# Shifting the tiles of a two-layer encoder kernel so that the two operands of every wide matmul start at the same offset modulo 512 bytes

## The chip, the cores and the metric

One Trainium2 chip; the program runs on one of its cores. The time is device microseconds of that core for one execution, and three executions of the kernel before are given. A profile of one more execution is read for the reasons.

## The reference, cut to what matters

Two layers over 1024 tokens of 1024 channels, all in float32. Each layer is a token mixer and a channel mixer, each between two RMS norms:

```
for l in range(DEPTH):                      # DEPTH = 2
    h = rmsnorm(x, g_pre_mix[l])
    z = h @ w_in[l]                         # 1024 -> 1536 columns
    y_f = fourier_mix(z[:, :256])           # 2-D DFT over positions and channels
    y_s = spatial_gating(z[:, 256:768])     # u * (W_s layernorm(v) + b), 4 heads, 128-token chunks
    y_a = gqa_attention(z[:, 768:])         # 8 query heads, 2 key/value heads of 64, rotary
    m = concat(rmsnorm(y_f), rmsnorm(y_s), rmsnorm(y_a)) * g_mix @ w_out[l]
    x = x + rmsnorm(m, g_post_mix[l])
    h = rmsnorm(x, g_pre_ffn[l])
    f = (silu(h @ w_gate[l]) * (h @ w_up[l])) @ w_down[l]    # 2816 hidden columns
    x = x + rmsnorm(f, g_post_ffn[l])
```

## The kernel before

Every float32 operand of a large product is kept as a pair (hi, lo) of float32r values, and a product is three matmuls, hi·hi, hi·lo and lo·hi (`matmul3`, line 142 of the profile). `matmul3` issues three times a pair of instructions: a load of a 128x128 stationary operand (the profile's engine PEld) and a matmul that streams a moving operand of 128x512 past it (PE). Nearly all of the kernel's time on the tensor engine is such matmuls. The loads run ahead, under the matmul before.

The stages of a layer, with the name that the profile gives to each stage's result tile:

- `z`: the input projection, three chunks of 512 columns by eight token tiles, 24 matmuls for each. The stationary operand is a piece of `hT` (transposed activations), the moving one a weight pair `w_z`. In the first chunk the transposes of the next token tile (`tp_h`) and of the keys (`ktp`) stand between the matmuls, in the third those of the Fourier and gating groups (`vf`, `yf`, `sv`, `ms`); the second chunk, for the queries, has none.
- attention: for each of 16 groups (token tile, kv head) of a layer and each of 8 key tiles, four transposes of exponentials (`ptr<-identr,pj`), two matmuls `pv<-pT,vv`, and, ahead for the next group, scores `sc<-kT,qT` in fours.
- `m`: the output projection, two runs of 24 matmuls for each token tile with transposes (`ytp`, `tp`) between them.
- gate and up (`fx`, `fy`): Strassen-Winograd products, 14 for each of 11 pairs of hidden tiles (7 variants by gate and up), 12 matmuls each. The stationary operand is a weight pair `w_f`, the moving one a variant of the activations: B11, B21, T1 (tiles `hB11`, `hB21`, `hT1`, on the left side of the memory) or T2, T3, T4, B22 (`hT2`, `hT3`, `hT4`, `hB22`, on the right). Of a pair's 168 matmuls 96 so have their moving operand on the right.
- down (`fX`, `fY`): Strassen-Winograd products whose operands `dw` lie in tiles of either side, with sums on POOL (`dr`), splits on ACT and DVE (`dw`) and accumulation on DVE (`nat`, line 1120).

Memory is given out by pools that grow from the left (low addresses) or the right (high addresses). A tile's size is rounded up to 32 bytes of a partition. Pools opened and closed as stacks reuse the same bytes, and a tile waits for the last use of the tiles that held its bytes. The order of instructions on each engine is set by the code, by `issue_after` constraints, and by the framework's planner (`schedule_with_timeline_sim=True`). The program's own table of tile addresses gives, in bytes of a partition:

```
tile                         address           mod 512   side
w_z, w_f, most w_wo (Wp)     57088 + 4096 i    256       left
raw tiles, first yT (rawp)   93952 + 4096 i    256       left
kT / vv / hB11 / hB21 / hT1  110336 ...        256       left
rf   (pool al)               134912            256       left, 32 bytes
qst, qT (pool al)            134944, 139040 .. 288       left, behind rf
vs, vsp (pool zs)            150336, 154432    320       left, behind rf and sgb
hT (z), hT2..hT4, hB22       163808 ... 212960 480       right
pT, half of the pj, oT       167904 ...        480       right
later yT, yFT, two w_wo      172000 ...        480       right
chm / ut, vt (pool fp)       170944 / 173024.. 448 / 480 right, mean (32 bytes) between
dw (down)                    both sides        256, 480  both sides
```

So the operands of a `z` matmul lie at 480 (stationary) and 256 (moving), those of T2, T3, T4 and B22 at 256 and 480, those of `pv` at 256 and 480, those of `sc` at 288 and 256, those of `m` mostly at 480 and 256, and those of B11, B21 and T1 both at 256. Of a layer's 924 `fX` and `fY` matmuls 624 have both at 256, 216 both at 480, and 84 have them apart, in runs of three.

The small tiles that the change touches: `one` (a column of ones, in pool `cst`), `mean` (a column of 1/256, set on POOL in `f_open`), `sgb` (the gating bias, loaded by SP after `sgg`), and `rf` (reciprocal roots of the Fourier group). `gz` and `gmx` are two rings of two 32-byte tiles in `cst`, each used once in a layer.

Of the kernel before, what the change touches and what calls it, by code (L numbers as in the profile page):

```python
# [27 lines left out]
# every float32 operand is a pair (hi, lo) of float32r values with x = hi + lo exactly;  # L28
# a product is hi.hi + hi.lo + lo.hi
# [3 lines left out]
def dft_constants():  # L33
    """Constants of the shapes alone: DFT factors and rotary angles."""
# [8 lines left out]
    # f > 0: real and imaginary part of the input give the outputs f; f = 0: two real inputs give the outputs 0 and 4  # L43
# [28 lines left out]
    def pair(v, axis):  # L72
        """(hi, lo): float32 constants as two float32r values."""
        v = v.astype(np.float32)
        hi = ((v.view(np.uint32) + np.uint32(0x800)) & np.uint32(0xFFFFF000)).view(np.float32)
        return np.ascontiguousarray(np.stack([hi, v - hi], axis))
# [5 lines left out]
def encoder_kernel(ctx, tc, A, out):  # L82
# [7 lines left out]
    st = pool("st", 6)  # L90
    nat = pool("natp").tile([P, NT, D], F32, name="nat")
# [14 lines left out]
    # besides ps1's four banks, four more as two pairs (key 2) or on their own (key 1)  # L106
# [8 lines left out]
    # ---------------- helpers  # L115
# [4 lines left out]
    def gain_split(w, raw, g):  # L120
        """(hi, lo) pair of raw with its rows scaled by g."""
        nc.scalar.activation(w[:, 0], raw, AF.Copy, scale=g)
        nc.vector.scalar_tensor_tensor(out=w[:, 1], in0=raw, scalar=g, in1=w[:, 0].bitcast(F32), op0=ALU.mult, op1=ALU.subtract)
# [6 lines left out]
    def wsplit(src, shape, name, p=None, **kw):  # L130
        """float32 in SBUF -> (hi, lo) pair."""
        w = (p or Wp).tile([P, 2] + shape, R32, tag="w", name=f"w_{name}", **kw)
        split(w[:, 0], w[:, 1], src)
        return w

    def rows2(w, r0, c0, n):
        """256 rows of a DRAM matrix as [128, 2, n]."""
        return w[r0:r0 + 256, c0:c0 + n].rearrange("(k p) n -> p k n", p=P)
# [16 lines left out]
    def unit_norm(x, n, name, pool=False):  # L155
        """x = x * rsqrt(mean(x^2) + eps), over the whole free range, in place."""
# [11 lines left out]
    def transpose_4(src, dst, o, name):  # L168
        """dst[:, hi/lo, k, o + tok] = src[tok, k*128 + .]^T for 128 tokens and 512 features."""
# [5 lines left out]
    class Residual:  # L175
        """x = src + rmsnorm(nat[:, t]) * gain, to DRAM; nat[:, t] = rmsnorm(x) * pre_gain, or x itself without a pre_gain.
        The columns of half eh are complete first."""
# [50 lines left out]
    class Later:  # L228
        """Work on the tensor engine that is issued some steps after what it depends on."""
# [16 lines left out]
    def behind(*engines):  # L246
        """Work that each of the engines issues after all that it has got so far."""
# [14 lines left out]
    def chain(*step):  # L262
        """A step that each engine issues after the previous step of the chain."""
# [14 lines left out]
    # ---------------- input projection's weights: three chunks of 512 columns  # L278
# [16 lines left out]
    def z_split(l, c, k):  # L295
        """The norm's gain belongs to the rows of the weights."""
# [4 lines left out]
    # ---------------- start  # L301
# [4 lines left out]
    one = cst.tile([P, 1], F32, name="one")  # L306
    nc.gpsimd.memset(one, 1.0)
    junk = cst.tile([P, 512], BF16, name="junk")
# [18 lines left out]
    # reciprocal roots of the tokens' mean squares: the norm before the input projection is applied to its output  # L327
# [24 lines left out]
    for l in range(DEPTH):  # L352
        gmx = cst.tile([P, 8], F32, tag="gmx", name=f"gmx{l}", bufs=2)
        nc.sync.dma_start(gmx, A["g_mix"][l].rearrange("(k p) -> p k", p=P))
        # ---------------- transposed, split activations (nat holds the pre-normalised tokens)
# [15 lines left out]
        # ---------------- input projection  # L371
# [13 lines left out]
        # queries carry the factor -1/8, so that a row's minimum is minus the maximum of its scaled scores  # L385
# [26 lines left out]
        def rope_apply(src, nh, which, t, dst, name, bufs, scale=1.0):  # L412
            """dst = src [P, nh, 64] times scale, normalised per head, gained and rotated."""
# [22 lines left out]
        # positions-mixed channels, keys and values  # L436
# [26 lines left out]
        # 8-point DFT over the token tiles, in place in nat[:, :, 0:256]  # L463
        def dft8():
# [10 lines left out]
            # xf: 0:e0 1:o0 2:e2 3:o2 4:e1 5:o1 6:e3 7:o3  # L475
            tt(t0, xf(0), xf(2), ALU.add)
            tt(t1, xf(0), xf(2), ALU.subtract)          # U2 real
            nc.vector.tensor_copy(xf(2), t1)
            tt(t1, xf(1), xf(3), ALU.subtract)          # -U2 imag
            tt(xf(3), xf(1), xf(3), ALU.add)  # L480
            tt(xf(0), t0, xf(3), ALU.add)               # U0
            tt(xf(1), t0, xf(3), ALU.subtract)          # U4
# [4 lines left out]
            stt(xf(5), t0, SQ, xf(4), ALU.add)          # U1 real  # L487
            stt(xf(7), t0, -SQ, xf(4), ALU.add)         # U3 real
            stt(xf(4), t1, SQ, xf(6), ALU.add)          # -U1 imag
            stt(xf(6), t1, -SQ, xf(6), ALU.add)         # U3 imag  # L490
# [4 lines left out]
        # queries  # L495
# [10 lines left out]
        sgb = zs.tile([P, 4], F32, name=f"sgb{l}")  # L506
        nc.sync.dma_start(sgb, A["sgu_b"][l].rearrange("h p -> p h"))

        # spatial gating: gelu, layer norm of the gate
# [28 lines left out]
        def gate_mul(i, j):  # L538
            """position mixing of token tiles 4i to 4i + 3, heads 2j and 2j + 1."""
# [12 lines left out]
        # position DFT runs between the second half's tiles  # L552
        fst = {}
        rf = al.tile([P, 8], F32, name=f"rf{l}")
# [8 lines left out]
        def f_open():  # L563
# [3 lines left out]
            fst["mean"] = fp.tile([P, 1], F32, name=f"mean{l}")  # L567
            nc.gpsimd.memset(fst["mean"], 1.0 / 256)
# [11 lines left out]
        def f_pos(f):  # L580
            """channel-major position transform; (channel half, real/imaginary, position), for f = 0 of the outputs 0, then 4."""
# [11 lines left out]
        def f_chan(f):  # L593
            """channel transform. The transform of real values at -k is the conjugate of the one at k."""
# [19 lines left out]
        def f_mean(f):  # L614
            """mean squares (+ eps) at the positions of y's two tiles, the same for both channel halves."""
# [15 lines left out]
        # ---------------- attention  # L631
# [5 lines left out]
        def yf_put(f1):  # L637
            """(hi, lo) of the transformed channels at the positions f1 + 8n; of those of a conjugate, backwards."""
# [11 lines left out]
        def y_tp(t, p=None):  # L650
            """transposed, split output of the gates and of the attention of token tile t."""
# [12 lines left out]
        def out_steps(t, oc, ps):  # L664
            """output projection of token tile t, a step for each 128 rows of the weights."""
# [13 lines left out]
        def wo_load(i):  # L679
            """i-th weight tile of the output projection in the order of use; the group norms' gains belong to its rows."""  # L680
# [117 lines left out]
        # scores and exponentials run ahead, by steps of a key tile  # L798
# [59 lines left out]
        # ---------------- output projection, post-norm, residual, pre-norm of the channel mixer  # L858
# [22 lines left out]
        def b_tp(t):  # L881
            """transposes token tile t's halves of the features, in place in nat; first variants of the right-hand operands."""
# [11 lines left out]
            else:  # L894
                nc.vector.tensor_tensor(out=half(u, 0), in0=ps[0], in1=half(u, 0), op=ALU.subtract)     # T1 = B12 - B11
                nc.scalar.copy(half(t, 1), ps[1])
                nc.vector.tensor_tensor(out=half(t, 0), in0=half(t, 1), in1=ps[0], op=ALU.subtract)     # T3 = B22 - B12

        # ---------------- channel mixer, gate and up: one level of Strassen-Winograd on
        # (output halves i0, i1) x (feature halves) x (token halves)  # L900
# [6 lines left out]
        def nb(i, j, u):  # L907
            """right-hand block (feature half i, token half j), token tiles 2u, 2u + 1 of the half."""
            return nat[:, 2 * u + 4 * j:2 * u + 4 * j + 2, i * 512:(i + 1) * 512]

        # variant and its place, and for some the difference that goes there; T4 is kept with the opposite sign
        TV = {"T1": ((0, 0),), "T2": ((0, 0), (1, 1), (0, 0)), "T3": ((0, 1),), "T4": ((1, 0), (1, 0), (0, 0)), "B22": ((1, 1),)}

        def t_sub(v, u, eng=nc.vector):
            """half u of variant v: T2 = B22 - T1, -T4 = B21 - T2."""
# [19 lines left out]
        def ff_sums(n):  # L935
            """Left-hand operands' sums of product n."""
# [7 lines left out]
            elif v == 3:  # L944
                tt(a21, a11, a21, ALU.subtract)         # S3 = A11 - A21
                tt(a11, sums[p, m], a11, ALU.subtract)  # S2 = S1 - A11
            elif v == 6:
                tt(a12, a12, a11, ALU.subtract)         # S4 = A12 - S2
# [12 lines left out]
        # in the order in which the right-hand operands' variants free nat  # L961
        PC = tuple((u, 0) for u in (4, 5, 6, 7, 0, 1, 2, 3)) + tuple((u, 1) for u in range(NT))

        def pc():
            """the next 2 KB slot for partial results, in nat's space."""
# [20 lines left out]
        def ff_post(n):  # L986
# [4 lines left out]
            def finish(key, acc, i, half):  # L991
                """gate or up block = acc + partial; after both, silu(gate) * up goes to DRAM."""
# [26 lines left out]
        # ---------------- channel mixer, down: Strassen-Winograd on (token halves) x (pairs of  # L1019
        # hidden tiles) x (column halves), groups of pairs accumulate in PSUM, then in nat  # L1020
# [11 lines left out]
        def d_raw_slot(gi, n):  # L1032
            """place of the n-th raw tile of group gi."""
            return RING[(12 * gi + n) % len(RING)]

        def d_load(gi, n):
            """n-th raw tile of a group: first tiles of the pairs, then second ones; hidden values, then weights."""
# [13 lines left out]
        def d_blk(gi, pi, side, b):  # L1051
            """quarter block b (row half * 10 + column half) of the left (side 0) or right factor."""
# [4 lines left out]
        def d_sums(gi, v):  # L1057
            for pi in range(len(DGROUPS[gi])):
# [3 lines left out]
                if v == 5:  # L1062
                    tt(a(11), a(11), a(21))             # S3 = A11 - A21
                    tt(a(21), a(21), a(22), ALU.add)    # S1 = A21 + A22
                    tt(w(11), w(12), w(11))             # T1 = B12 - B11
# [242 lines left out]
```

## Time and profile before

| what | value |
|---|---|
| three executions | 2302.60, 2304.02, 2301.32 us (median 2302.6) |
| profiled execution, first to last instruction (the page gives its own time by this span alone) | 2305.6 us |
| PE busy | 2219.3 us (96%), 10460 matmuls and transposes |
| DVE, ACT, POOL busy | 1601.5, 1139.0, 953.2 us (69, 49, 41%) |
| mean granted TensorE clock | 0.983 |

The busy time of PE is a union of pipelined intervals: a 128x512 matmul is shown with 390 to 480 ns, while the next one starts 227 to 235 ns after it. What a run of matmuls costs is read from start to start in the order of time, so: the start of the group behind it less its own start, divided by its count.

### The profile page before, as it was taken

How to read it: one execution, taken by the hardware profiler on the slowest of the kernel's cores; microseconds unless marked ns; L12 is line 12 of the kernel's file. 1: busy time of each engine (PE TensorE's matmuls, PEld its weight loads, DVE VectorE, ACT ScalarE, POOL GpSimd, SP SyncE). 2: the span in 40 equal slices, each digit the busy share in tenths (PEclk: the TensorE clock that was granted, in tenths of full speed). 3: DMA queues.
4: the chain of work that ended last, by engine and by line, in shares of the span. 5: the costliest groups of instructions: out<-in, count | busy, mean ns of one | idle time of the engine just before them, and what ended most of it. 6: DMA issues, size and time to landing. Idle time of an engine off the chain costs nothing. (4 is left out here: it accounts for less than half of the span.)

```text
span 2305.6 us, 29160 instructions
## 1 busy us (share of the span) xinstructions
PE 2219.3 (96%) x10460; PEld 1806.0 (78%) x10460; DVE 1601.5 (69%) x2457; ACT 1139.0 (49%) x2188; POOL 953.2 (41%) x798
## 2 busy tenths in 40 slices
PE   9999999999999999999899999999999999999986
PEld 7787888878888888777677788888788888877774
DVE  6868986585444447899977598865844444488998
ACT  6337996553333334533452489855533333344333
POOL 2632442242313135656636235332432323266556
PEclk9999999999999999999999999999999999999998
DMA  4110003213222226321231000042132323262212
GB/s 157 42 44 19 16 13 112 100 64 98 67 93 72 86 76 229 120 83 46 93 115 46 17 19 19 10 137 83 60 101 73 92 68 97 65 233 110 83 46 110
DMA packets 104962, 185.28 MB, mean 80 GB/s; under 512 B 12273, under 2 KB 62705, under 8 KB 104817
## 3 DMA queue, kind: packets, MB, share of 16 engines
q1 hardware_dynamic: 103376, 178.70, 22.8%
q0 software_dynamic: 1440, 4.72, 0.7%
q8 instruction: 82, 1.34, 0.2%
q14 instruction: 64, 0.52, 0.1%
HBM read 143.54 MB, written 39.85 MB: 80 GB/s over the span
## 5 line engine op out<-in xcount | busy, mean ns | idle before, releaser
L142 PE MATMUL fx<-hT,w_f 128*128 128x512 f32 x1584 | 386.4, 400 | 6.7 <-ACT nat L1003 4.5
L142 PEld LDWEIGHTS fx<-hT,w_f 128*128 128x128 f32 x1584 | 301.1, 190 | 81.2 <-ACT nat L1003 6.0
L118 DVE TENSOR_TENSOR w_f<-raw_f,w_f 128x512 fp32r<-128x512 f32 x264 | 207.7, 791 | 201.3 <-ACT w_f L117 197.8
L118 DVE TENSOR_TENSOR dw<-dr,dw 128x512 fp32r<-128x512 f32 x300 | 324.5, 1126 | 31.0 <-ACT dw L117 30.7
L142 PE MATMUL z<-w_z,hT 128*128 128x512 f32 x1152 | 289.8, 404 | 12.5 <-DVE rz L194 5.1
L117 ACT CAST dw<-dr 128x512 fp32r<-128x512 f32 x308 | 171.9, 618 | 235.3 <-POOL dr L1061 92.1
L117 ACT CAST w_f<-raw_f 128x512 fp32r<-128x512 f32 x264 | 162.1, 621 | 239.6 <-PE fy L142 199.5
L142 PEld LDWEIGHTS z<-w_z,hT 128*128 128x128 f32 x1152 | 213.9, 191 | 65.0 <-DVE rz L194 5.5
L142 PE MATMUL fX<-dw,dw 128*128 128x512 f32 x1056 | 249.9, 392 | 8.6 <-DVE nat L1120 8.3
L142 PE MATMUL fy<-hB,w_f 128*128 128x512 f32 x1056 | 251.5, 393 | 0.9 <-DVE hB L118 0.9
L940 POOL TENSOR_TENSOR s<-raw_f,raw_f 128x512 f32<-128x512 f32 x44 | 58.0, 1318 | 466.6 <-DMA raw_f<-in_w_gate_dram 431.4
L142 PEld LDWEIGHTS fX<-dw,dw 128*128 128x128 f32 x1056 | 197.0, 188 | 56.0 <-DVE nat L1120 13.7
L142 PEld LDWEIGHTS fy<-hB,w_f 128*128 128x128 f32 x1056 | 198.0, 188 | 46.2 <-DVE hB L118 1.7
L1061 POOL TENSOR_TENSOR dr<-dr,dr 128x512 f32<-128x512 f32 x132 | 220.3, 1698 | 8.6 <-DVE dw L118 8.6
L142 PE MATMUL fY<-dw,dw 128*128 128x512 f32 x792 | 200.0, 410 | 22.2 <-DVE nat L1120 18.6
L994 DVE TENSOR_TENSOR nat<-fy,nat 128x512 f32<-128x512 f32 x132 | 90.9, 690 | 182.8 <-ACT nat L1003 92.1
L142 PEld LDWEIGHTS fY<-dw,dw 128*128 128x128 f32 x792 | 156.7, 199 | 61.3 <-DVE nat L1120 20.2
L118 DVE TENSOR_TENSOR pT<-ptr,pT 128x512 fp32r<-128x512 f32 x256 | 171.8, 685 | 36.1 <-ACT pT L117 33.6
L749 PE MATMUL pv<-pT,vv 128*128 128x512 f32 x512 | 181.6, 436 | 0.3 <-DVE pT L118 0.3
L1003 ACT COPY nat<-fx 128x512 f32<-128x512 f32 x132 | 77.4, 586 | 193.6 <-PE fx L142 187.9
L117 ACT CAST pT<-ptr 128x512 fp32r<-128x512 f32 x256 | 150.7, 596 | 40.2 <-PE ptr L737 37.9
L720 DVE TENSOR_REDUCE mx<-sc 128x1 f32<-128x1024 f32 x128 | 156.0, 1220 | 12.0 <-PE sc L717 9.8
(208 smaller groups left out, 3754.0 us busy)
## 6 DMA issues: line engine op xcount, KB each, us to landing
raw_f<-in_w_gate_dram SPq DMA_DIRECT2D x44, 512.0 KB, 3.6
raw_f<-in_w_up_dram SPq DMA_DIRECT2D x44, 512.0 KB, 4.0
asp<-nat SPq DMA_DIRECT2D x88, 256.0 KB, 2.6
dr<-in_w_down_dram SPq DMA_DIRECT2D x44, 512.0 KB, 6.1
dr<-asp SPq DMA_DIRECT2D x44, 512.0 KB, 6.6
xin<-xs SPq DMA_DIRECT2D x24, 512.0 KB, 3.3
raw_z<-in_w_in_dram SPq DMA_DIRECT2D x16, 512.0 KB, 4.5
raw_wo<-in_w_out_dram SPq DMA_DIRECT2D x16, 512.0 KB, 3.8
```

The lines of the kernel that those rows point to most:

```text
L117: nc.scalar.copy(hi, src)
L118: eng.tensor_tensor(out=lo, in0=src, in1=hi.bitcast(F32), op=ALU.subtract)
L142: nc.tensor.matmul(ps, lhs(a), rhs(b), start=first and i == 0, stop=last and i == 2, **kw)
L720: nc.vector.tensor_reduce(mx, sc, axis=AX.X, op=ALU.min)
L749: nc.tensor.matmul(pv, vv[:, kt, g].rearrange("p i d -> p (i d)"), pT[:, i], start=(kt == 0 and i == 0), stop=(kt == 7 and i == 1))
L940: tt = lambda o, x, y, op: nc.gpsimd.tensor_tensor(out=o, in0=x, in1=y, op=op)
L994: nc.vector.tensor_tensor(out=t, in0=acc, in1=t, op=ALU.add)
L1003: nc.scalar.copy(t, X)
L1061: tt = lambda o, x, y, op=ALU.subtract: nc.gpsimd.tensor_tensor(out=o, in0=x, in1=y, op=op)
```

## The change

A tile `edge` of 56 float32 (224 bytes) is taken first on the right side and never used. `one` and `mean` become the two columns of a tile `scal`; `mean` is set once at the start and `fp`'s own `mean` goes. `sgb` moves from pool `zs` into the ring `gmx`, `rf` from pool `al` into the ring `gz`. Comments are removed; the arithmetic is the same.

```diff
+    pool("edge", 1, "right").tile([P, 56], F32, name="edge")
...
-    one = cst.tile([P, 1], F32, name="one")
+    scal = cst.tile([P, 2], F32, name="scal")
+    one, mean = scal[:, 0:1], scal[:, 1:2]
     nc.gpsimd.memset(one, 1.0)
+    nc.gpsimd.memset(mean, 1.0 / 256)
...
-        sgb = zs.tile([P, 4], F32, name=f"sgb{l}")
+        sgb = cst.tile([P, 8], F32, tag="gmx", name=f"sgb{l}", bufs=2)[:, 0:4]
...
-        rf = al.tile([P, 8], F32, name=f"rf{l}")
+        rf = cst.tile([P, 8], F32, tag="gz", name=f"rf{l}", bufs=2)
...
-            fst["mean"] = fp.tile([P, 1], F32, name=f"mean{l}")
-            nc.gpsimd.memset(fst["mean"], 1.0 / 256)
+            fst["mean"] = mean
```

## Rows read from the trace of the kernel before

**Rows 1.** The page: its span, and from its first part PE's busy time, share of the span and instructions.

```profile
span 2305.6 us, 29160 instructions
PE 2219.3 (96%) x10460; PEld 1806.0 (78%) x10460; DVE 1601.5 (69%) x2457; ACT 1139.0 (49%) x2188; POOL 953.2 (41%) x798
```

**Rows 2.** Groups of instructions on PE by line and operation, shapes kept apart: out<-in, shapes, count | busy us, mean ns of one | idle us before, and what ended it.

```profile
L142 PE MATMUL fx<-hT,w_f 128*128 128x512 f32 x1584 | 386.4, 400 | 6.7 <-ACT nat L1003 4.5 <-DVE hT L118 2.2
L142 PE MATMUL z<-w_z,hT 128*128 128x512 f32 x1152 | 289.8, 404 | 12.5 <-DVE rz L194 5.1 <-DVE ra_q L425 2.6 <-DVE w_z L123 2.3
L142 PE MATMUL fy<-hB,w_f 128*128 128x512 f32 x1056 | 251.5, 393 | 0.9 <-DVE hB L118 0.9
L749 PE MATMUL pv<-pT,vv 128*128 128x512 f32 x512 | 181.6, 436 | 0.3 <-DVE pT L118 0.3
L717 PE MATMUL sc<-kT,qT 128*128 128x512 f32 x512 | 146.0, 409 | 7.9 <-ACT pj L730 7.2 <-ACT qT L707 0.7
L142 PE MATMUL m<-w_wo,yT 128*128 128x512 f32 x576 | 143.3, 399 | 0.5 <-ACT yT L117 0.5
L142 PE MATMUL m<-w_wo,yFT 128*128 128x512 f32 x192 | 50.6, 397 | 0.0
```

**Rows 3.** The order of time on PE in one pair of the second layer's gate and up: start us, length us, line, operation, count. `fy<-hB` at 1708.18 is variant B21, `fy<-hB` at 1740.46 is B22.

```profile
1707.26 1.09 PE L142 MATMUL fx<-hB,w_f 128*128 128x512 f32 x4
1708.18 5.61 PE L142 MATMUL fy<-hB,w_f 128*128 128x512 f32 x24
1713.63 5.60 PE L142 MATMUL fy<-hT,w_f 128*128 128x512 f32 x24
1719.07 5.76 PE L142 MATMUL fx<-hT,w_f 128*128 128x512 f32 x24
1724.67 2.45 PE L142 MATMUL fx<-hB,w_f 128*128 128x512 f32 x10
1726.96 5.76 PE L142 MATMUL fx<-hT,w_f 128*128 128x512 f32 x24
...
1740.46 5.76 PE L142 MATMUL fy<-hB,w_f 128*128 128x512 f32 x24
1746.06 1.09 PE L142 MATMUL fx<-hB,w_f 128*128 128x512 f32 x4
```

**Rows 4.** Busy time of the engines in a stretch of one pair's length: the stretch, its length, busy us (count) of PE, PEld, DVE, ACT and POOL, granted TensorE clock, DMA share, GB/s.

```profile
1719.23:1758.03 38.80, 38.80 (x170) 31.55 (x169) 17.00 (x24) 13.89 (x24) 11.28 (x8) 1.00 0.27 82
```

**Rows 5.** The order of time on PE near the end of the first layer's down stage; the operands of the 14 all lie at 480 on the right side, those of the four all at 256.

```profile
1122.91 1.09 PE L142 MATMUL fY<-dw,dw 128*128 128x512 f32 x4
1123.84 3.36 PE L142 MATMUL fX<-dw,dw 128*128 128x512 f32 x14
```

**Rows 6.** The order of time on PE in the first layer's input projection, chunk one (at 43 us), two (76 us) and three (129 us).

```profile
43.45 3.50 PE L142 MATMUL z<-w_z,hT 128*128 128x512 f32 x14
46.79 0.60 PE L172 MATMUL tp_h<-identr,nat 128*128 128x128 f32 x4
...
76.72 33.06 PE L142 MATMUL z<-w_z,hT 128*128 128x512 f32 x141
...
129.48 11.47 PE L142 MATMUL z<-w_z,hT 128*128 128x512 f32 x48 [0.18 <-ACT gv L516]
```

**Rows 7.** The order of time on PE in the first layer's attention.

```profile
339.42 0.71 PE L749 MATMUL pv<-pT,vv 128*128 128x512 f32 x2
339.97 1.09 PE L717 MATMUL sc<-kT,qT 128*128 128x512 f32 x4
340.90 0.60 PE L737 MATMUL ptr<-identr,pj 128*128 128x128 f32 x4
```

**Rows 8.** The order of time on PE in the first layer's output projection.

```profile
409.28 4.44 PE L142 MATMUL m<-w_wo,yT 128*128 128x512 f32 x18
413.56 1.56 PE L142 MATMUL m<-w_wo,yFT 128*128 128x512 f32 x6
414.96 1.03 PE L888 MATMUL tp<-identr,nat 128*128 128x128 f32 x8
```

**Rows 9.** Busy time of the engines, as in rows 4, in four stretches: end of the first layer's input projection chunk two, its attention, its down stage, and the turn from gate and up to down in the second layer.

```profile
57.00:116.50 59.50, 57.59 (x256) 45.76 (x254) 47.85 (x115) 21.04 (x40) 37.28 (x31) 1.00 0.13 40
220.00:361.00 141.00, 141.00 (x872) 119.26 (x871) 127.90 (x180) 129.03 (x248) 58.73 (x65) 1.00 0.04 12
926.00:1100.00 174.00, 164.17 (x687) 133.00 (x687) 156.99 (x182) 70.79 (x129) 102.47 (x61) 0.95 0.22 79
2040.00:2070.00 30.00, 28.40 (x124) 22.87 (x122) 28.75 (x25) 15.71 (x29) 27.54 (x18) 1.00 0.53 201
```

**Rows 10.** What PE waited for: who waited for whom, us in total, times, longest us.

```profile
PE fY L142 <- DVE nat L1120: 18.6, 6, 4.7
...
PE sc L717 <- ACT pj L730: 7.2, 6, 1.8
...
PE z L142 <- DVE ra_q L425: 2.6, 2, 1.3
```

**Rows 11.** The chain of work that ended last, at the turn from gate and up to down in the second layer: start us, length us, what.

```profile
2057.05 11.87 POOL dr L1061 x7
```

**Rows 12.** The instructions that write `mean`: duration ns (least, median, most), first and last start us.

```profile
L568 POOL MEMSET mean<- x2: 120/120/120, 136.2 to 1280.6; 128x1 f32 x2
```

## The prediction

> **What bounds the kernel now.** I read the page first, for which engine is full: PE is busy for 2219.3 of 2305.6 us [rows 1], so the kernel is a queue of matmuls with 86 us of holes. Second, the groups by line, for which matmuls these are [rows 2]: the seven groups shown alone hold 5,584 of the 10,460, all with 512 columns. Third, the order of time, because the busy time cannot tell what one matmul costs: only the distance from one start to the next can.
>
> There the reader is to see two step lengths in one stage under the same conditions. In gate and up, 24 matmuls `fy<-hT` (T1) reach from 1713.63 to 1719.07, 5.44 us or 226.7 ns each; the next 24, `fx<-hT` (T2), from 1719.07 to 1724.67, 5.60 us or 233.3 ns each [rows 3]. [...] What differs is the address: T1 lies at 256 modulo 512 like its weights, T2 at 480. B22, also at 480, takes 5.60 us (1740.46 to 1746.06), B21, at 256, takes 5.45 (1708.18 to 1713.63) [rows 3]. So apart costs 6.7 ns a matmul more.
>
> It is not the right side of the memory as such: 14 matmuls of the down stage with both operands at 480 on the right take 3.36 us to the end of the last [rows 5]. Less one matmul's 0.39 us (the mean of the like group `fy` [rows 2]) this is 2.97 us for 13 steps, 228.5 ns each.
>
> The same rows show that the short step is not there at once. The 14 lose 0.02 us against 13 steps of 226.7 (2.95 us); four matmuls with both operands at 256, after an interruption, take 0.93 us from 1122.91 to 1123.84, against 0.907 [rows 5]; the ten of B11 behind T2 take 2.29 us, 229.0 ns each, from 1724.67 to 1726.96 [rows 3]. I cost an aligned run of n matmuls as 226.7 n + 25 ns and one apart as 233.3 n. A run so gains 6.7 n - 25 ns: 136 for 24, 68 for 14, 15 for 6, 2 for 4, and nothing for 2.
>
> **What the change does to the addresses.** 56 floats are 224 bytes, and 480 - 224 = 256, the left side's value. With `rf` and `sgb` gone, `qst` and `qT` go from 288 to 256 and `vsp` from 320 to 256; with `mean` gone, `chm` does so too. All pairs are then equal. The shift takes no room that is in use: `hT1` ends at 163584 and the lowest right-hand tile begins at 163808, just 224 bytes above.
>
> **Gate and up.** From 1707.26 to 1746.06 is one pair, 38.80 us [rows 3]. 168 matmuls of 226.7 ns are 38.08, so a pair gains 0.72 us: 0.64 from the 96 on the right and 0.08 from B11, which need no longer settle behind them. 22 pairs: 15.8 us. Not all of it arrives. In each layer's first pair T2 runs between waits for ACT and DVE (6.7 us in all [rows 2]): 24 x 6.7 ns x 2 = 0.3 is lost. At the turn to down, seven sums of POOL, 11.87 us, stand on the chain [rows 11], and DVE and POOL are busy for 28.75 and 27.54 of 30 us [rows 9]. I write off the last ten products before it, of which eight lie on the right: 96 x 6.7 ns x 2 = 1.3.
>
> **Input projection.** Chunk two runs without interruption: 141 matmuls in 33.06 us [rows 6], less 0.40 for the last [rows 2], are 233.3 ns a step. 384 matmuls of two layers gain 2.6 us. In chunk one a token tile is cut into runs of 4, 14 and 6 (the 14 and the cut behind them stand in [rows 6]): 2 + 68 + 15 ns, by 16 tiles 1.4 us. Chunk three has runs of 48 [rows 6] down to one and is put between them, 1.9. Together 5.9. Chunk two ends in waits for DVE's rotary work, up to 1.3 us each [rows 10], where DVE is busy for 47.85 of 59.5 us [rows 9]; a faster PE waits longer there, and I take 0.5 us a layer away.
>
> **Output projection.** A run is 18 + 6 matmuls from 409.28 to 414.96 [rows 8]. 768 matmuls [rows 2] are 32 runs, of which about three are cut up: 29 x 136 ns = 3.9 us.
>
> **Attention.** `sc` stands in fours: 339.97 to 340.90 is 0.93 us [rows 7], just what four aligned ones took above. `pv` stands in twos. I take 0.3 us for 128 fours. The bounds: nothing, and 6.4 us if the short step came at once (512 x 5.8 + 512 x 6.7 ns).
>
> **Down.** 168 matmuls apart are worth 1.1 us, but DVE is busy for 156.99 of 174 us [rows 9] and PE waits for its accumulation for 18.6 us [rows 10]. I take half, 0.5; the bounds are 0 and 1.1.
>
> **The moved small tiles.** Two memsets of 120 ns [rows 12] leave POOL's middle, and one of the same kind comes at the start, where the first input tiles are still being loaded; without that cover it costs 0.12 us. The rings now turn in the order `gz`, `rf` and `gmx`, `sgb`. `gmx1` so waits for the last reader of `gmx0`, `gz1` for that of `gz0`, both hundreds of us earlier; behind them on SP stand the weight loads, which therefore do not wait. `sgb`'s own load keeps its place behind `sgg`'s. By the address table no shifted tile comes to lie on a former tile that it did not lie on already; a few lose such a neighbour. Nothing on either side.
>
> **The sum.** 15.8 + 5.9 + 3.9 + 0.3 + 0.5 = 26.4, less 0.3 + 1.3 + 1.0, is 23.8 us. From the profiled 2305.6 that leaves 2281.8 us; that execution stands 3.0 us over the median of the runs, and from 2302.6 it leaves **2279 us**.
>
> **Rivals.**
>
> *Nothing moves.* The two steps could come from something else that goes with T2 to B22, and the offset would be a bystander: then the time stays at 2302.6. Against it, the 14 on the right at equal offsets and chunk two's `z`, whose sides are exchanged (stationary on the right) and whose step is long [rows 5, 6]. [...] Chance 0.05.
>
> *The others take it back.* Only what arrives from gate and up stays, 15.8 - 1.6 = 14.2 us, because ACT and DVE, 129.03 and 127.90 of 141 us in attention [rows 9], and DVE elsewhere set the pace: 2288. For it, the waits in [rows 10]; against it, PE is busy for all 141 us there. Chance 0.15.
>
> *The short step comes at once, and all of it arrives.* The groups of [rows 2] count 1584 + 528 (half of `fy<-hB`) + 1152 + 576 + 512 + 512 = 4864 matmuls; by 6.7 ns 32.6 us, with 1.1 for down and 1.8 for B11 35.5: 2267. Against it, the fours and tens of [rows 3, 5]. Chance 0.15.
>
> *Slower: the planner reorders attention.* The order is planned from simulated times and dependencies, some of which the moved tiles change. If each of the 30 groups that follow the first of a layer had one more wait of `sc` for ACT's exponentials, of the mean 1.2 us (7.2 by 6 [rows 10]), that is 36 us: 2302.6 - 23.8 + 36 = 2315. It decides from 0.8 us a group. For it, ACT's 129.03 of 141 us; against it, PE's 141.00 there and no new dependency. Chance 0.03.
>
> **The numbers.** The forecast has the remaining 0.62. The low end, 2267, is the third rival's; the high end, 2291, the second's with one more wait of 1.3 us a layer. Inside lie the forecast and most of these two, some 0.86; nothing narrower holds 8 in 10, because attention alone may add 6 us and the other engines may keep 10. About 0.2%, 4.6 us, is what a measurement of this kernel can tell from no change. Faster holds the forecast and the rivals two and three, 0.92; same 0.05; slower 0.03.
>
> **What would show it.** In the profile after, 24 `fx<-hT` from start to start take 5.44 us instead of 5.60, and a pair takes 38.08; `z` in chunk two has a step of 226.7 ns; `sc` in fours stays at 0.93 (0.907 would speak for the third rival); the waits of PE for DVE in chunk two and in down are longer by half a microsecond or more in each layer; no wait on POOL's `mean` or on SP's `sgb`. Wrong it would be if `fx<-hT` kept its 233 ns, if the steps fell but the stages' lengths did not, or if attention's order had changed.

## The result, and the profile after

The changed kernel takes 2283.84 us (median of five runs, 2282.25 to 2286.03), the kernel before on the same chip 2303.85 (five runs, 2301.32 to 2307.5). The ratio is 0.9914, with a 95% interval of 0.9901 to 0.9928. Two more comparisons of the same kernels, each beside other runs of before, gave 0.9909 (0.9894 to 0.9923) and 0.9895 (0.9881 to 0.991). So the change takes away some 19 to 24 us, about 1%. Forecast were 2279 and a gain of 23.8 us: the sign, the place and the mechanism held, and this gain of 20.0 us came out below the sum.

The page, first its span and PE, DVE, ACT and POOL, as in [rows 1]:

```profile
span 2280.5 us, 29159 instructions
PE 2191.5 (96%) x10460; PEld 1807.2 (79%) x10460; DVE 1607.3 (70%) x2457; ACT 1138.5 (50%) x2188; POOL 952.2 (42%) x797
```

PE lost 27.8 us of busy time, and no other engine's changed by more than 5.8 us (DVE, 1601.5 before). PE still executes its 10,460 matmuls in the order of before. The two spans differ by 25.1 us, more than the medians by 5: the profiled execution of before is the slowest of its five runs (its span and the 1.9 us around it make 2307.5), that of after the fastest. What that does to the comparison is said under "The whole" below; a stage's gain is good to one or two us.

The group `z` of [rows 2], in the same columns:

```profile
L144 PE MATMUL z<-w_z,hT 128*128 128x512 f32 x1152 | 286.3, 403 | 11.8 <-DVE rz L196 5.1 <-DVE ra_q L429 4.6 <-ACT w_z L124 1.0
```

`z` lost 3.5 us of busy time, and PE's idle time before it for `ra_q` (a step of the queries' rotary work on DVE) rose from 2.6 to 4.6.

The order of time on PE, one stretch each of the input projection, the output projection, attention and gate and up, answering to [rows 3, 6, 7, 8]; start us, length us, what, and in brackets the idle time before it:

```profile
73.82 33.79 PE L144 MATMUL z<-w_z,hT 128*128 128x512 f32 x148
109.92 15.28 PE L144 MATMUL z<-w_z,hT 128*128 128x512 f32 x58 [2.31 <-DVE ra_q L429]
...
338.26 1.09 PE L720 MATMUL sc<-kT,qT 128*128 128x512 f32 x4
339.18 0.60 PE L740 MATMUL ptr<-identr,pj 128*128 128x128 f32 x4
...
391.84 4.35 PE L144 MATMUL m<-w_wo,yT 128*128 128x512 f32 x18
396.03 1.53 PE L144 MATMUL m<-w_wo,yFT 128*128 128x512 f32 x6
397.40 1.03 PE L891 MATMUL tp<-identr,nat 128*128 128x128 f32 x8
...
1688.93 1.07 PE L144 MATMUL fx<-hB,w_f 128*128 128x512 f32 x4
...
1700.71 5.60 PE L144 MATMUL fx<-hT,w_f 128*128 128x512 f32 x24
1706.15 2.43 PE L144 MATMUL fx<-hB,w_f 128*128 128x512 f32 x10
1708.42 5.60 PE L144 MATMUL fx<-hT,w_f 128*128 128x512 f32 x24
...
1727.01 1.07 PE L144 MATMUL fx<-hB,w_f 128*128 128x512 f32 x4
```

T2 (`fx<-hT`) now goes from 1700.71 to 1706.15: 5.44 us, the length that T1 had before [rows 3]. B11's ten take 2.27 us, 227 ns each, for they no longer settle behind T2. The pair from 1688.93 to 1727.01 is 38.08 us against 38.80 [rows 3], 0.72 less. A run of 18 + 6 in the output projection takes 5.56 us (391.84 to 397.40) against 5.68 [rows 8]. Four `sc` take 0.92 us against 0.93 [rows 7].

PE's order is the same in both traces, so the gain of a stage is the distance between the same two matmuls in the one less that in the other. Gate and up is counted to its last product (the first six products of down stand among its last sixty):

| stage | layer 1, us | layer 2, us | both | in the sum |
|---|---|---|---|---|
| input projection, chunk one | 0.98 | 0.27 | 1.25 | 1.4 |
| chunk two, to its last product | 1.15 | 1.11 | 2.26 | 2.6 |
| chunk three, with the wait at its head | 0.05 | 0.09 | 0.14 | 1.9 less 1.0 |
| attention | 2.24 | -0.68 | 1.56 | 0.3 |
| output projection | 1.67 | 1.69 | 3.36 | 3.9 |
| gate and up | 8.05 | 7.62 | 15.67 | 15.8 less 1.6 |
| down | 0.49 | 0.33 | 0.83 | 0.5 |
| all | | | 25.1 | 23.8 |

Chunk three gained next to nothing. PE's order of time at its head, before:

```profile
75.01 34.77 PE L142 MATMUL z<-w_z,hT 128*128 128x512 f32 x148
111.09 1.89 PE L142 MATMUL z<-w_z,hT 128*128 128x512 f32 x7 [1.31 <-DVE ra_q L425]
113.58 3.30 PE L142 MATMUL z<-w_z,hT 128*128 128x512 f32 x13 [0.60 <-DVE w_z L123]
117.42 7.96 PE L142 MATMUL z<-w_z,hT 128*128 128x512 f32 x33 [0.54 <-DVE w_z L123]
```

The 148 start 1.19 us earlier in the changed kernel and take 0.98 us less, but PE then waits 2.31 us for the rotary sum `ra_q` instead of 1.31. The engines around that wait, in columns as in [rows 4] (the granted clock is the third number from the end), before and then after:

```profile
110.00:115.00 5.00, 3.31 (x13) 2.44 (x14) 4.66 (x10) 2.38 (x4) 4.01 (x5) 1.00 0.18 52
```

```profile
110.00:115.00 5.00, 5.00 (x15) 3.71 (x16) 5.00 (x10) 2.37 (x4) 4.89 (x3) 0.66 0.18 52
```

Before, the clock stays at 1.00. After, it averages 0.66 over these 5 us: 0.50 in each of the three from 111 to 114, 0.81 and 0.98 in the two beside them. That is 3.4 us at 0.50, right behind a stretch in which PE had been idle for 2.31 us. PE's two later waits for `w_z`, 0.60 and 0.54 us before, are gone: PE works at this lower clock while DVE splits the next weights, instead of waiting for them. DVE's order of time shows the three splits after whose last PE goes on, before (PE's matmul at 117.42) and then after (the same matmul is at 116.26, inside the 58):

```profile
114.26 3.10 DVE L123 SCALAR_TENSOR_TENSOR w_z<-raw_z,gz,w_z 128x512 fp32r<-128x512 f32 x3
```

```profile
113.08 3.11 DVE L125 SCALAR_TENSOR_TENSOR w_z<-raw_z,gz,w_z 128x512 fp32r<-128x512 f32 x3
```

The splits end at 117.36 and 116.19, 6.3 us behind the end of `ra_q` in both, and the matmul follows within 0.1 us in both. So up to there DVE sets the pace, and the fall of the clock cost no time: this matmul comes 1.15 us earlier than before, the first one behind the wait 1.18. In the second layer they are 15.10 and 15.08.

Why `ra_q` does not come sooner, its instructions of chunk two in DVE's order of time show (after; the first stands at 71.69):

```profile
78.01 0.69 DVE L429 TENSOR_TENSOR ra_q<-z,rh_q 128x512 f32<-128x512 f32 x1 [2.04 <-POOL rh_q L428]
84.36 0.69 DVE L429 TENSOR_TENSOR ra_q<-z,rh_q 128x512 f32<-128x512 f32 x1 [2.04 <-POOL rh_q L428]
95.03 0.69 DVE L429 TENSOR_TENSOR ra_q<-z,rh_q 128x512 f32<-128x512 f32 x1 [1.82 <-POOL rh_q L428]
102.65 0.68 DVE L429 TENSOR_TENSOR ra_q<-z,rh_q 128x512 f32<-128x512 f32 x1
109.17 0.69 DVE L429 TENSOR_TENSOR ra_q<-z,rh_q 128x512 f32<-128x512 f32 x1 [1.25 <-POOL rh_q L428]
```

One token tile's rotary round, handed between DVE and POOL, takes 6.35 us, and did so before. Two of the five rounds here are longer, 10.67 and 7.62 us: the first DFT (`dft8`, 11.9 us of DVE's work) stands for the most part in them. The five take 37.5 us in both kernels. PE made a tile's 24 products in 5.60 us and makes them in 5.44 now. It was ahead of the rounds already, and a faster PE only stands longer at the end of the chunk: it comes there 2.17 us earlier than before, `ra_q` 1.17.

### The profile page after: what moved, and what is told of

It reads as the page before. It is cut to its first block, busy times and chain, and to the rows that moved or that the text cites. A ratio compares the mean times of both kernels' runs of the same rounds, so it can differ in the third digit from the quotient of the medians.

```text
span 2280.5 us, 29159 instructions
## 1 busy us (share of the span) xinstructions
PE 2191.5 (96%) x10460; PEld 1807.2 (79%) x10460; DVE 1607.3 (70%) x2457; ACT 1138.5 (50%) x2188; POOL 952.2 (42%) x797
## 5 line engine op out<-in xcount | busy, mean ns | idle before, releaser
L144 PE MATMUL fx<-hT,w_f 128*128 128x512 f32 x1584 | 374.9, 393 | 6.6 <-ACT nat L1006 4.5
L120 DVE TENSOR_TENSOR w_f<-raw_f,w_f 128x512 fp32r<-128x512 f32 x264 | 213.9, 814 | 192.6 <-ACT w_f L119 189.5
L144 PE MATMUL fY<-dw,dw 128*128 128x512 f32 x792 | 198.3, 408 | 24.1 <-DVE nat L1123 19.3
```

Source lines behind the costliest of these rows:

```text
L120: eng.tensor_tensor(out=lo, in0=src, in1=hi.bitcast(F32), op=ALU.subtract)
L144: nc.tensor.matmul(ps, lhs(a), rhs(b), start=first and i == 0, stop=last and i == 2, **kw)
```

## The experiments

**e1_steps: the step itself.** A kernel of its own that has only matmuls, 48 of one kind behind another, and a copy of the input as its output. One tile holds everything; its distances are set by hand:

```
def section(name, m, s, count=48, n=512, step=P):
    o = bank(name)
    for j in range(count):                  # moving at m floats, stationary at 4096 + s
        mm(o, m, 4096 + s + (j % 4) * step, n)
...
for d in range(16):                         # 32 bytes more from one to the next
    section("r" + L[d], 8 * d, 0)
...
```

> This kernel leaves out the encoder: it copies x to the output and, beside that, issues runs of 48 matmuls of 128x512 out of one tile, whose moving operand lies 0, 32, 64 ... 480 bytes further than the stationary one (sections ra to rp), then 4, 8 and 16 bytes further (fa to fc), then both 32, 128, 224 and 480 bytes on (ea to ed), 256 and 128 columns equal and 224 bytes apart (ne, nx, qe, qx), stationary operands alternately equal and 224 bytes apart (own, off), and runs of twelve behind four transposes, equal (te) and apart (tx). Offset theory (only the difference modulo 512 counts): 226.7 ns a step for ra, zero, warm and ea to ed, about 233 ns for at least the differences of 224 and 288 bytes (rh, rj); what the others take is open. Place theory (an operand is slow where it does not start at 256 modulo 512, or on a coarse boundary): ea to ed differ among each other, and equal operands are not always short. Runs of twelve behind transposes: te gains 6.7 x 12 - 25 = 55 ns on tx.

Its order of time (`ra` 0 bytes apart, `rb` 32, `rc` 64, `rd` 96, `rh` 224, `ri` 256, `rj` 288, `rk` 320, `rl` 352; `fa` 4, `fb` 8; `eb` both operands at 128, `ec` both at 224; `te` and `tx` twelve behind four transposes, equal and apart):

```profile
39.47 11.04 PE L38 MATMUL ra<-big 128*128 128x512 f32 x48
50.35 11.37 PE L38 MATMUL rb<-big 128*128 128x512 f32 x48
61.55 11.16 PE L38 MATMUL rc<-big 128*128 128x512 f32 x48
72.55 11.37 PE L38 MATMUL rd<-big 128*128 128x512 f32 x48
...
117.39 11.35 PE L38 MATMUL rh<-big 128*128 128x512 f32 x48
128.58 11.05 PE L38 MATMUL ri<-big 128*128 128x512 f32 x48
139.47 11.37 PE L38 MATMUL rj<-big 128*128 128x512 f32 x48
150.67 11.16 PE L38 MATMUL rk<-big 128*128 128x512 f32 x48
161.67 11.37 PE L38 MATMUL rl<-big 128*128 128x512 f32 x48
...
228.59 11.52 PE L38 MATMUL fa<-big 128*128 128x512 f32 x48
239.94 11.35 PE L38 MATMUL fb<-big 128*128 128x512 f32 x48
...
273.18 11.09 PE L38 MATMUL eb<-big 128*128 128x512 f32 x48
284.11 11.09 PE L38 MATMUL ec<-big 128*128 128x512 f32 x48
...
344.95 3.00 PE L38 MATMUL te<-big 128*128 128x512 f32 x12
347.78 0.60 PE L72 MATMUL tr<-id,big 128*128 128x128 f32 x4
348.14 3.04 PE L38 MATMUL tx<-big 128*128 128x512 f32 x12
351.01 0.60 PE L72 MATMUL tr<-id,big 128*128 128x128 f32 x4
```

From one start to the next, by 48: equal 10.88 us or 226.7 ns (39.47 to 50.35), 32 bytes apart 11.20 us or 233.3 ns, 224 bytes apart 233.1. The kernel's two lengths stand here alone, with nothing beside them but the address. What nobody had forecast is the period: 256 bytes apart is as good as equal (10.89 us), and 320 is again what 64 is (11.00 us for both, 229 ns). The diff's modulus of 512 is twice what counts. From single starts, without each section's first ten, distances of 0 and 64 give 226.7 and 228.9 ns, 160 and 416 bytes 234.2, and the other multiples of 32 bytes 233.3 to 233.5; 16 bytes apart gives 231.7, and 4 bytes apart costs more than any other, 11.35 us or 236.5 ns. Equal operands give 226.7 ns at whatever place they lie; `eb` and `ec` (10.93 us) are longer by what they take to settle, some nine matmuls. `ri`, behind a section with unequal operands, has the short step from its second matmul on, so how long settling takes is not explained by the section before. Twelve behind transposes gain 0.04 us by equal offsets (2.83 against 2.87), where 0.055 was expected. With 256 columns equal offsets gain nothing: 48 (`ne` and `nx`, 224 bytes apart) take 5.91 us equal and 5.84 apart.

**e2_edge_only and e3_small_only: the change in two parts.** The first has the padding alone, the second the removed and re-homed small tiles alone.

```
+    pool("edge", 1, "right").tile([P, 56], F32, name="edge")     # e2: before and this line
-    pool("edge", 1, "right").tile([P, 56], F32, name="edge")     # e3: after without it
```

> The unused 224 bytes on the right alone; one, mean, sgb and rf stay where they were before, so that qT stays 32 bytes off and vsp, vs and chm stay off too. Offset theory: all but about 1 us of the whole change's gain, 18 to 21 us faster than before (2282 to 2286); fx<-hT steps of 226.7 ns and a pair of 38.08 us. Small-tiles theory (the gain comes from the moved small tiles and the waits on former tiles that go with them): within 2 us of before.

> All of the change but the 224 unused bytes: one and mean in one tile, sgb and rf in the rings; the right side stays at 480. Offset theory: within 2 us of before, pairs of 38.80 us. Small-tiles theory: most of the 20 us.

The padding alone takes 2285.67 us, ratio 0.9919 (0.9904 to 0.9934); the small tiles alone 2303.22, ratio 1.0001 (0.9991 to 1.0012). T2 and B11 in e2, and T2 and the ten behind it in e3:

```profile
1703.28 5.60 PE L143 MATMUL fx<-hT,w_f 128*128 128x512 f32 x24
1708.72 2.43 PE L143 MATMUL fx<-hB,w_f 128*128 128x512 f32 x10
```

```profile
1718.17 5.76 PE L143 MATMUL fx<-hT,w_f 128*128 128x512 f32 x24
1723.78 2.45 PE L143 MATMUL fx<-hB,w_f 128*128 128x512 f32 x10
```

5.44 and 5.61 us from start to start. So one line carries the whole gain that can be measured, and the small tiles neither cost nor bring anything beyond 0.1%.

**e4_left_pad: the place or the distance.** The same 224 bytes at the left edge, so that every operand lies at 480 instead of 256.

```
-    pool("edge", 1, "right").tile([P, 56], F32, name="edge")
+    pool("edge", 1, "left").tile([P, 56], F32, name="edge")
```

> The change with its 224 unused bytes on the left instead of the right: all operands then lie at 480 modulo 512. Offset theory: as the whole change, 2281 to 2287 us, pairs of 38.08 us. Place theory (256 modulo 512 is the good place): slower than before, since the pairs that were equal at 256 now lie at 480 too; pairs of 39.2 us (168 steps of 233.3 ns) and a time of 2307 us or more.

2284.69 us, ratio 0.9917 (0.9901 to 0.9934), and T2 has the short length:

```profile
1703.96 5.60 PE L144 MATMUL fx<-hT,w_f 128*128 128x512 f32 x24
1709.40 2.43 PE L144 MATMUL fx<-hB,w_f 128*128 128x512 f32 x10
```

It is the distance between the two operands, not the place of either.

**e8_edge_40: half the way.** 160 bytes of padding put the right side at 320, 64 bytes from the left one modulo 256.

```
-    pool("edge", 1, "right").tile([P, 56], F32, name="edge")
+    pool("edge", 1, "right").tile([P, 40], F32, name="edge")
```

> The change with 160 instead of 224 unused bytes on the right: the right side lies at 320, 64 bytes behind the left one modulo 256. By the steps measured on their own: gate and up, whose moving operand is the one on the right, take the step of 228.9 ns for their 96 matmuls a pair (pair of 38.3 us), and the input projection, where the stationary operand is the one on the right (the moving one 192 bytes further modulo 256), keeps 233.4 ns: some 11 us faster than before. If only equal offsets count and nothing between: pairs of 38.80 us and the time of before.

```profile
74.24 34.77 PE L144 MATMUL z<-w_z,hT 128*128 128x512 f32 x148
110.38 1.90 PE L144 MATMUL z<-w_z,hT 128*128 128x512 f32 x7 [1.37 <-DVE ra_q L429]
...
1701.33 1.09 PE L144 MATMUL fx<-hB,w_f 128*128 128x512 f32 x4
...
1713.16 5.67 PE L144 MATMUL fx<-hT,w_f 128*128 128x512 f32 x24
1718.67 2.48 PE L144 MATMUL fx<-hB,w_f 128*128 128x512 f32 x10
...
1739.82 1.09 PE L144 MATMUL fx<-hB,w_f 128*128 128x512 f32 x4
```

T2's 24 take 5.51 us, 229.6 ns each: e1's middle class shows in the whole kernel. A pair takes 38.49 us (1701.33 to 1739.82), between 38.80 and 38.08, and the one run 2298.59, 5.3 us under the median of before (2303.93) and 3.2 under its lowest. In chunk two, where moving and stationary change sides and the distance is 192 instead of 64, the 148 keep their 34.77 us. The sign of the distance counts, as in e1, where 64 gave 228.9 ns and 192 233.4. The gain is less than was expected: the pair was put at 38.3 us without the steps that settle behind unequal operands, and a ten of B11 takes 2.32 us here (1718.67 to 1720.99) instead of 2.27. The 0.19 us of a pair make 4 of the 6 us that are missing; the rest, in a single run, stays open.

**e5_after_again, e6_dft_t1, e7_dft_t0: is the longer wait a backlog?** DVE has an extra piece of work, the first DFT, among the rotary rounds of chunk two. If it were what makes `ra_q` late, an earlier place for it would shorten the wait. e5 is the changed kernel again, beside them.

```
-            if t == 2:
+            if t == 1:                     # e6; t == 0 in e7
                 dft8()
```

> The changed kernel once more, for the runs beside it. 2282 to 2286 us, 0.9914 of before within 0.0015. Both theories on the input projection: its chunk two ends in one wait of z for DVE ra_q of 2.3 us in each layer, and the granted clock lies at 0.5 for some microseconds behind it, or behind the waits at the start of attention.

> The changed kernel with the 8-point transform dft8 (25 DVE instructions, some 12 us of DVE) issued after token tile 1 of chunk two instead of tile 2. Theory that the DVE backlog at the end of chunk two ate what the input projection gained: the wait of 2.3 us in each layer shrinks below 1 us, the clock does not fall there, and the time is 3 to 8 us under the changed kernel's. Rival (the rotary chain itself, DVE waiting for POOL's rh_q, sets that wait): the wait stays over 1.5 us and the time within 2 us.

> As the run before, with dft8 issued after token tile 0 of chunk two, so that one more tile's time stands between it and the end of the chunk. Backlog theory: the wait is gone and the time another 0 to 3 us lower. Rival: as above.

2284.81, 2284.62 and 2287.75 us, ratios 0.9909 (0.9894 to 0.9923), 0.9907 (0.9891 to 0.9924) and 0.9922 (0.9906 to 0.9937). In e6:

```profile
109.66 15.49 PE L144 MATMUL z<-w_z,hT 128*128 128x512 f32 x59 [2.25 <-DVE ra_q L429]
```

The wait is 2.25 us instead of 2.31, in e7 2.24, and there PE waits for `w_z` besides, 0.96 us and in the second layer 0.70. So an earlier place does not help. That does not clear the extra work itself: in both kernels it still stands ahead of the `ra_q` that PE waits for, and the five rounds take 37.4 us in e6 and 37.9 in e7, as against 37.5. By an estimate from the rows, five rounds of 6.35 us without it would take 31.8, and the wait would go. A kernel with the DFT behind the sixth tile was not run, so whether that saves time is open.

**e9_rope_add, e10_rope_both, e11_after_beside: can the wait be had back?** e9 moves the round's last addition from POOL to DVE, e10 its scaling too; e11 is the changed kernel beside them.

```
-            nc.gpsimd.tensor_tensor(out=dst, in0=b, in1=c, op=ALU.add)
+            (nc.vector if nh == 8 else nc.gpsimd).tensor_tensor(out=dst, in0=b, in1=c, op=ALU.add)
...
-            nc.gpsimd.tensor_tensor(out=r, in0=r, in1=scale.to_broadcast([P, 8]), op=ALU.mult)
+            nc.vector.tensor_scalar_mul(r, r, scale)                       # e10 alone
```

> The changed kernel with the last addition of the queries' rotary step (nat<-rb_q,rc_q, 1.3 us on POOL) on DVE. In the changed kernel a token tile's round of that step takes 6.35 us (ra_q on DVE to the next ra_q), of which POOL has 4.6 us, while PE needs 5.44 us for the tile. Theory that this round sets the wait at the end of chunk two: the round falls under 5.44 us, the wait of 2.3 us in each layer goes, the clock does not fall there, and the time is 4 to 9 us under the changed kernel's, near 2277 us. Rival (DVE is full enough that 8 more additions of some 0.7 us a layer only move the wait on): within 2 us of the changed kernel.

> As the run before, with the multiplication of the queries' roots by the tokens' roots (rh_q, 0.2 us on POOL with its hand-overs) on DVE too. Theory: one hand-over less in the round; 0 to 2 us under the run before. Rival: the same as the run before.

> The changed kernel beside these two: 2282 to 2287 us, 0.991 of before.

2285.26, 2284.69 and 2282.99 us, ratios 0.9899 (0.9884 to 0.9914), 0.9897 (0.9881 to 0.9914) and 0.9895 (0.9881 to 0.991): no difference. In e9:

```profile
109.48 1.19 PE L144 MATMUL z<-w_z,hT 128*128 128x512 f32 x4 [0.81 <-DVE ra_q L429]
112.38 12.95 PE L144 MATMUL z<-w_z,hT 128*128 128x512 f32 x43 [1.71 <-DVE w_z L125]
```

The wait for `ra_q` falls to 0.81 us, and 1.71 us of waiting for DVE's split of the weights `w_z` come in its place; together they are longer than the 2.31 us that went. The five rounds take 36.0 us here, so the wait for `ra_q` follows the rounds; but DVE has both jobs, and the time does not follow. In e10 PE waits 2.23 and 0.89 us in the first layer, 1.93 and 0.79 in the second. No version faster than the changed kernel was found.

## Why the prediction was right, and where its sizes were off

**Gate and up: right to the hundredth in a pair, the deductions too large.** A pair was put at 38.08 us and takes 38.08. All eight undisturbed pairs together went from 310.40 to 304.64 us in each layer, 0.72 a pair. Net of the two deductions the sum had 14.2 us, and the trace has 15.7, of which some 0.6 are the clock's (an estimate: what the first pair gained more in the first layer than in the second). The 1.3 written off at the turn to down was not lost: the last pair gained 0.83 in each layer. The first two pairs were put at 1.29 a layer and gained 1.46 in the first, where the granted clock was at 0.50 for 3.4 instead of 6.8 us at the stage's start, and 1.03 in the second. The sum lacked a wait there: at the head of the second pair PE waits 1.01 and 0.87 us for DVE's part of `hB` (the lo value of a variant of the activations) instead of 0.44 and 0.42.

**The rival "nothing moves" fell.** e1 and e4 leave no bystander: the same instruction, the same place, only another distance, 226.7 against 233.3 ns, in e1 at a mean granted clock of 1.00. The runs do not show why the distance of the two operands counts, only that the step depends on it.

**The rival "at once" fell as well.** Four `sc` take 0.92 us instead of 0.93, not the 0.907 it needed, and te against tx shows 0.04 us on twelve. The settling term, 25 ns a run, was about right: the 18 + 6 of the output projection gain 0.12 us where 0.136 was put, so 3.4 instead of 3.9.

**The rival "the others take it back" fell too.** By it only gate and up's gain would have stayed; the output projection kept 3.4 us and the input projection 3.65, and the waits grew by 1.0 us a layer for `ra_q`, by some 0.5 for `hB` and by 0.35 for down's accumulation.

**The input projection was mis-sized.** Sum: 5.9 less 1.0, that is 4.9. Trace: 1.25 + 2.26 + 0.14 = 3.65. Chunks one and two gained about what was put. What was too small is the 0.5 us a layer that a faster PE would wait longer: it waits 1.00 longer (2.31 against 1.31). The rounds of 6.35 us and more were there to be read before, on DVE's order of time; against PE's 5.60 us a tile they say that all of chunk two's gain goes into the wait, not half of it. Behind the wait the stage then gains 1.03 us (the same matmul is 1.18 us earlier at the one end and 2.21 at the other), near the 0.95 a layer that was put.

One thing was not foreseen at all: behind the longer wait the clock falls to 0.50, for 3.4 us in each layer. It cost nothing here, because DVE's splits of `w_z` set the pace in that stretch, as shown above. That it is the wait that brings the clock down is argued from the kernels set side by side: every kernel with a wait for `ra_q` of 2.2 us or more shows the fall behind it (from 110 to 114 us the clock averages 0.58 after, 0.57 in e4 and 0.58 in e6), and before, e3 and e8, with 1.3 to 1.4 us, do not (1.00 in the same stretch of before and e3); e9, whose idle time is cut in two, shows it in the first layer (0.81 and 1.71 us; 0.50 from 112 to 116) and not in the second (0.38 and 1.68), and e10 shows it in the second too, behind 1.93 us. A run that lengthens nothing but this wait was not made.

**Attention: right apart from the clock.** In its steady part 0.3 us a layer were gained (0.3 for both was put). The rest, 1.9 us gained in the first layer and 1.0 lost in the second, all falls on the first scores of each layer. There the clock was at 0.50 for 6.8 us (first layer) and 3.4 us (second) before, and for none and 6.8 us after. This goes with the arrangement and is not chance of one execution: all three profiles of the changed kernel have none and 6.8 us, while e3 has 6.8 and e8 3.4 us in the first layer, and both 3.4 in the second. e4 has the same offsets and 6.8 us in both, so it does not follow from the offsets alone; what decides it is open. The order of the work did not change, and the slower rival fell.

**Down: 0.8 us instead of 0.5,** inside the bounds of 0 and 1.1. PE's wait for its accumulation grew from 18.6 to 19.3 us, 0.35 a layer, less than the half microsecond that was named as a sign.

**The whole.** The profiled pair shows 25.1 us where the sum had 23.8. The clock gave about 1.5 of them (1.9 - 1.0 at the first scores, 0.6 in the first layer's first pair), which was not in the sum; without it the stages add up to 23.6, with the input projection 1.25 below its term and gate and up 0.9 above. That the sum is so close is partly luck, since these two errors nearly cancel.

The medians show 20.0, 19.1 and 24.0 us in three comparisons. Of the 4.8 us between 2279 and 2283.84, 1.25 is the median of before itself, which rose from 2302.6 to 2303.85 with more runs. The rest is of the size of what goes with the clock of the runs. Runs of before at a mean granted clock of 0.987 took 2300.5 to 2303.0 us, those at 0.983 took 2307.5 to 2309.3. The profiled execution of before had 0.983, but the median run of before had 0.985 in the comparison that shows 19.1, and 0.984 in the one that shows 24.0. The changed kernel's runs lie at 0.981 to 0.984. So the two profiles stand side by side at much the same clock (two falls of 3.4 us in that of after cost nothing), and the medians do not. Why the clock differs from run to run is open. (The prediction puts the profiled execution 3.0 us over the median; it compares a span with a time. The execution took 2307.5, 4.9 over it. The 2279 comes from the median and does not hang on this.)

## What to carry to other kernels

Where a stream of wide matmuls loads new weights for each, look at the addresses: the same instruction with two step lengths in one undisturbed stage, read from start to start, is the sign (226.7 and 233.3 ns here), and here one padding tile at the edge of the memory brought the whole gain that can be measured (e2, ratio 0.9919). Small tiles allocated ahead of large ones move everything behind them by their size; what brought the short step to 512-column matmuls in e1 was a distance of the two operands that is a multiple of 256 bytes (48 take 10.88 us at 0 and 10.89 at 256, against 11.20 at 32); at 256 columns, equal offsets gained nothing. Before a gain is counted, lay the producer's time for a tile beside the round of the engines that consume it: where the round is longer, as here with 6.35 against 5.60 us a tile, the gain turns into a wait (the first layer's chunk two is 1.15 us shorter here, the wait behind it 1.00 us longer). And before a fall of the clock behind a wait is counted as a loss, see whether PE would have had to wait in that stretch anyway, as it did here for the splits of `w_z` (0.60 and 0.54 us before).

## What the runs showed of the hardware that was not expected

- In e1 the step of a 512-column matmul with a new weight for each depends on (moving - stationary) modulo 256 bytes: 226.7 ns at 0, 228.9 at 64, 234.2 at 160, 233.3 to 233.5 at the other multiples of 32, 231.7 at 16 and 236.5 at 4 bytes. The sign counts: 64 (228.9) is good, 192 (233.4) is not. Why is open.
- In `eb` and `ec` the short step needed some nine equal matmuls to set in (10.93 us for 48, where `ra` takes 10.88), in `ri` one (10.89); on what that depends is open. Equal and unequal ones in turn, 24 of them in e1, do not reach it: their steps are 233.3 ns on average.
- At 256 columns equal offsets are not better (5.91 against 5.84 us for the 48 of `ne` and `nx` in e1).
- At one place of the input projection a wait of 2.2 to 2.3 us on PE stood ahead of 3.4 us or more at a granted clock of 0.50 in every kernel that had it (0.58 on average from 110 to 114 us in the changed kernel), one of 1.3 to 1.4 us in none (1.00 there before). In the changed kernel the fall cost no time, since DVE set the pace there: its splits of `w_z` end at 116.19 us, at 117.36 before.
